# Two-block transformer on one core: last token rows turned inside the next part's first products, input loads reordered, output product in other PSUM banks

## The chip, the cores and the metric

The kernel runs on one core of a Trainium2 chip. The metric is the device time of one execution in microseconds, as the median of three runs; lower is better.

## The reference, cut to what matters

512 tokens of width 1024 go through a first block (a layer norm, then two layers, each a mixer followed by an MLP) and a second block (two layers over 16 meta tokens and the 512 tokens, 528 columns). What is computed at the places where one part follows another:

```python
x = layer_norm(x, ln0_g, ln0_b)
for l in range(DEPTH):                       # first block
    mix = hybrid_mixer(x, w_in[l], ...)      # ends with merged @ w_out[l]
    x = layer_norm(alpha * x + mix, ln1_g[l], ln1_b[l])
    hid = jnp.square(jax.nn.relu(x @ w_up[l]))
    x = layer_norm(alpha * x + hid @ w_down[l], ln2_g[l], ln2_b[l])
...
for l in range(DEPTH):                       # second block
    h = h + mixer2(rmsnorm(h, norm_g[l]), ...) @ w_out_2[l]
out = rmsnorm(h, final_g)
```

## The kernel before, in words

**Layout.** Between parts the tokens lie in rows: four tiles of 128 tokens by 1024 features, called token tiles 0 to 3 here (the second block has a fifth tile of 16 meta tokens, in front). A product needs them turned, features on the partitions: `to_features` (L190 to L197) turns one token tile with eight 128 by 128 transposes on TensorE (line L196) into two PSUM tiles. ScalarE rounds each into `xh` (L120), and VectorE writes the rest into `xl` (L121), so that a float32 product is three fast ones (xh by the high weight, xl by the high weight, xh by the low weight; `mm3`, line L107). Weights come by DMA into a ring of three buffers `wraw`, and `wsplit` makes the two parts: `whi` on ScalarE (L85), `wlo` on VectorE, or on GpSimd for the first tiles of a part (L87).

**Places where one part follows another.** The program is one long list, and the Tile compiler assigns buffers, waits and, by its own model of readiness, the order of each engine's queue. Where these places are:

- *Start* (`input_norm`, L278): x and the two layer norm rows (spread over 128 partitions by the DMA) are loaded, each token tile is normalized on VectorE (`layer_norm`: statistics L204, gain L210, bias L211) and turned, the parameter rows are loaded and turned (`params`, L325), and the first weights come after all that on the same DMA queue, SP's.
- *M0, M1* (`mixer` to `mlp`, layers 0 and 1): the mixer ends with `gated`, which multiplies each product by its gate (`th`, L576), adds to `acc` on GpSimd (L578) and splits the sum into `mh`, `ml`. The out product (L1000) then runs with tokens as output rows: its first 512 columns for all four token tiles while weights stream in, then its second 512 columns token tile by token tile, with residual add (L1004), layer norm and turning of each. The turning of token tile 3 comes after its layer norm.
- *O0, O1*: the beginning of that out product, behind the last products of `gated`. Its eight PSUM tiles are one ring of the pool `wop` (all eight banks). The mixer's product tiles `mm` are two banks of the pool `pm`, closed just before.
- *L0* (`mlp` to the next `mixer`) and *L1* (`mlp` to the second block): the down product (L1079) ends token tile by token tile in eight banks, with add (L1118), layer norm and turning. At L1 a root-mean-square norm (`rms`, L1151 to L1158) stands between.
- *P0* (second block, `project` of layer 0 to `feed` of layer 1): the same with L1686 and L1691, and `norm_tile`.

Each of the five then starts with `gemm_halves`: the first two weight tiles of the next part are multiplied with the first half of the token columns (256 of 512; 264 of 528 in the second block), then with the second half, 96 products in all. The first half reads token tiles 0 and 1 alone (and the meta rows).

```python
for h in range(2):                              # gemm_halves, L388
    hs = slice(256 * h, 256 * h + 256)
    for w, ps in zip(ws, tiles):
        self.b.mm3([(ps[:, hs], hs)], w, (self.xh, self.xl), nk, start=(h == 0))
```

- *N0, N1* (`latent` in the second block, L1395): five products of small width are normalized together. Two steps of another chain (`fox`: its q and k products) are handed out, and then, in two parts, a row of factors is spread (`rb`, L1440, VectorE), turned into PSUM (`bc`, L1444, TensorE) and multiplied in. `fox` goes on after both, with its v product. Products and `bc` share two PSUM buffers of two banks each.

In the mixers and the second block a planner written out in Python (`Weave`) decides the order in which chains of work are handed out: each chain yields an estimate of its TensorE time and of the delay until it can go on.

Of the kernel before, what the change touches and what calls it, by code (L numbers as in the profile page):

```python
# [15 lines left out]
P = 128  # L16
# [13 lines left out]
class B:  # L30
# [59 lines left out]
    def wstream(self, src, nk, c0, ntiles, m=P, spare=0):  # L90

        i = 0
        while i < ntiles:
            g = min(1024 // (nk * m), ntiles - i)
            raw = self.wload(src, nk, c0 + i * m, g * m)
# [118 lines left out]
def row_bcast(b, pool, vec, tag):  # L214
    t = b.t(pool, [P, vec.shape[0]], tag, bufs=1)
    b.nc.sync.dma_start(t, vec.unsqueeze(0).to_broadcast([P, vec.shape[0]]))
    return t


class First:  # L220


    def __init__(self, b, ctx, x_last):
        self.b, self.nc, self.a, self.tc = b, b.nc, b.a, b.tc
        nc, a, tc = self.nc, self.a, self.tc
        k1 = ctx.enter_context(tc.tile_pool(reuse_waits="tile", name="k1", bufs=1))
        self.res_d = [b.dp.tile([4, P, D], F32, name=f"res{i}") for i in range(DEPTH)]
        self.xh, self.xl = b.xh[:, :, :S], b.xl[:, :, :S]
        self.x_last = x_last
        self.PT = b.t(k1, [P, 95], "PT")  # L230
# [50 lines left out]
    def input_norm(self):  # L281
        b, nc, a, tc = self.b, self.nc, self.a, self.tc
        with ExitStack() as c2:
            tp = c2.enter_context(tc.tile_pool(reuse_waits="tile", name="ln0", bufs=1))
            pp = c2.enter_context(tc.tile_pool(reuse_waits="tile", name="ln0p", bufs=2, space=PSUM, side="right"))
            zs = [b.t(tp, [P, D], "z", bufs=4) for tt in range(4)]
            nc.sync.dma_start(zs[0], a["x"][0, 0:P, :])
            gb = row_bcast(b, tp, a["ln0_g"], "gb")
            bb = row_bcast(b, tp, a["ln0_b"], "bb")
            for tt in range(1, 4):  # L290
                nc.sync.dma_start(zs[tt], a["x"][0, tt * P : (tt + 1) * P, :])
            nc.sync.dma_start(b.ident, a["c_ident"])
            prm = self.params(0, tp, pp, "tr")
            next(prm)
            for tt, z in enumerate(zs):
# [302 lines left out]
    def low_rank(self, rp):  # L598
        b, nc = self.b, self.nc
        ws = b.wstream(self.w_in, KD, ZR + 1536, 3, spare=2)  # L600
        early = self.gemm_halves([next(ws), next(ws)])
# [343 lines left out]
    def mixer(self, l):  # L945
# [7 lines left out]
        accp = mctx.enter_context(tc.tile_pool(reuse_waits="tile", name=f"acc{l}", bufs=1))  # L953
        acc = b.t(accp, [P, KD, S], "acc")
# [36 lines left out]
        with ExitStack() as c2:  # L991
            wp = c2.enter_context(tc.tile_pool(reuse_waits="tile", name=f"wo{l}", bufs=1))
            pp = c2.enter_context(tc.tile_pool(reuse_waits="tile", name=f"wop{l}", bufs=8, space=PSUM))
# [34 lines left out]
            for tt in range(4):  # L1028
                pt = b.t(pp, [P, S], "b")
# [7 lines left out]
            to_features(b, pp, "b", x, self.xh, self.xl, tt * P)  # L1037
# [6 lines left out]
    def mlp(self, l):  # L1044
# [4 lines left out]
        with ExitStack() as c2:  # L1049
# [9 lines left out]
            with ExitStack() as c3:  # L1059
                self.pm = c3.enter_context(tc.tile_pool(reuse_waits="tile", name=f"up{l}", bufs=4, space=PSUM))  # L1060
                ws = b.wstream(a["w_up"][l], KD, 0, FF, spare=2)
                early = self.gemm_halves([next(ws), next(ws)])
# [41 lines left out]
            gb = row_bcast(b, hq, a["ln2_g"][l], "gb")  # L1104
            bb = row_bcast(b, hq, a["ln2_b"][l], "bb")
            if last:
                g2 = row_bcast(b, hq, a["norm_g_2"][0], "g2")
                norm_tile(b, hq, pp, "b", 4, g2)()
            for tt in range(4):
# [9 lines left out]
                layer_norm(b, hq, x, gb, bb, x)  # L1119
                if last:  # L1120
                    turn = norm_tile(b, hq, pp, "b", tt, g2)
                else:
                    nc.sync.dma_start(self.res_d[l + 1][tt], x)
                    turn = partial(to_features, b, pp, "b", x, self.xh, self.xl, tt * P)
            turn()
# [20 lines left out]
def rms(b, pool, h, n, gb, half=None):  # L1146
    nc = b.nc
    hn = b.t(pool, [P, D], "hn", bufs=2)
# [13 lines left out]
def norm_tile(b, pool, pp, tag, i, gb, half=None):  # L1162
    h, n, col = h_tile(b, i)
    hn = rms(b, pool, h, n, gb, half)
# [15 lines left out]
class Second:  # L1180
# [216 lines left out]
    def latent(self, l, cp, ps0, ws):  # L1397
# [40 lines left out]
        for part, tiles in ((0, range(3)), (1, range(3, 5))):  # L1438
# [11 lines left out]
            yield 1.2, 0.0  # L1450
# [216 lines left out]
    def project(self, l):  # L1667
# [3 lines left out]
        with ExitStack() as c2:  # L1671
# [55 lines left out]
            if turn:  # L1727
                turn()


def build(tc, a, out, stop=None, dbg=None):
    with ExitStack() as ctx:
# [11 lines left out]
        def open_residual():  # L1744
            hp = ctx.enter_context(tc.tile_pool(reuse_waits="tile", name="h2", bufs=1, side="right"))
            b.h_tok = b.t(hp, [P, 4, D], "htok")
            b.h_meta = b.t(hp, [NM, D], "hmeta")
            nc.sync.dma_start(b.h_meta, a["meta_tokens_2"])
# [90 lines left out]
```

## Time and profile before

| | |
|---|---|
| median of three runs | 3620.09 us (3615.1 to 3625.79) |
| the profiled execution, its own time | 3614.28 us |
| span in the trace | 3612.5 us |
| TensorE matmul busy | 3430.6 us (95%) |
| VectorE / ScalarE / GpSimd busy | 1891.6 / 1220.2 / 559.2 us |
| mean granted TensorE clock | 0.974 of full speed |

A trace row of the timeline has the start in us from the span's start, the duration, the engine, the source line and operation, output and inputs, and, in brackets, how long the engine had been idle before and what released it. A matmul's duration overlaps with the next one's, so work per product is read as the distance of starts, or from a stretch in which TensorE is never idle.

### The profile page before, as it was taken

The page shows a single profiled execution, that of the slowest core. Times are in us where ns is not written, and L with a number is a line of the kernel's source. Part 1 is how long each engine was busy: PE and PEld are TensorE (multiplying, and loading weights), DVE is VectorE, ACT ScalarE, POOL GpSimd, SP SyncE. Part 2 cuts the span into 40 slices and gives each one's busy share as a digit, 9 for nine tenths or more (in the row PEclk, how much of TensorE's full clock was granted, in tenths as well). Part 3 has the DMA queues.
Part 4 walks back from the last instruction along what each step waited for, and adds up shares of the span by engine and source line. Part 5 has one row for each costly group of instructions (what it writes and reads, how often), then busy time and mean ns, then how long its engine had stood idle before and what let it go on. Part 6 is the DMA issues. An engine that isn't in the chain of part 4 may idle for free. (4 is left out here: it accounts for less than half of the span.)

```text
span 3612.5 us, 56238 instructions
## 1 busy us (share of the span) xinstructions
PE 3430.6 (95%) x22346; PEld 2747.3 (76%) x22346; DVE 1891.6 (52%) x4547; ACT 1220.2 (34%) x2339; POOL 559.2 (15%) x660
## 2 busy tenths in 40 slices
PE   7999999999999989989989999899999999999998
PEld 5666676678887766667768888878989977787787
DVE  6576674552235556765552235465465355655634
ACT  2333342222223333423222223344333234443422
POOL 2221120222201211111122200110000111100011
PEclk9999999999999999999999999999999999999999
DMA  5422223333334322223342334122222332222232
GB/s 176 114 65 65 74 64 105 111 119 94 94 94 128 94 79 61 70 63 94 111 138 81 95 93 138 38 51 65 66 65 71 88 80 45 62 58 66 71 88 93
DMA packets 471832, 309.37 MB, mean 86 GB/s; under 512 B 105085, under 2 KB 433797, under 8 KB 471569
## 3 DMA queue, kind: packets, MB, share of 16 engines
q1 hardware_dynamic: 470992, 303.68, 30.0%
q8 instruction: 176, 2.88, 0.3%
q0 software_dynamic: 576, 2.10, 0.1%
q14 instruction: 88, 0.71, 0.1%
HBM read 280.76 MB, written 24.95 MB: 85 GB/s over the span
## 5 line engine op out<-in xcount | busy, mean ns | idle before, releaser
L107 PE MATMUL mm<-xh,whi 128*128 128x512 f32 (+2 forms) x3024 | 1002.9, 362 | 2.9 <-ACT whi L85 1.7
L107 PE MATMUL mm<-xh,wlo 128*128 128x512 f32 (+2 forms) x3024 | 969.4, 352 | 8.7 <-DVE wlo L87 7.3
L107 PE MATMUL mm<-xl,whi 128*128 128x512 f32 (+2 forms) x3024 | 972.7, 353 | 0.0
L87 DVE TENSOR_TENSOR wlo<-wraw,whi 128x1024 fp32r<-128x1024 f32 (+3 forms) x454 | 526.2, 1159 | 648.3 <-ACT whi L85 609.0
L85 ACT ACTIVATE whi<-wraw 128x1024 fp32r<-128x1024 f32 (+2 forms) x466 | 452.5, 971 | 1101.3 <-PE mm L107 835.6
L107 PEld LDWEIGHTS mm<-xh,whi 128*128 128x128 f32 x3024 | 540.9, 191 | 102.2 <-issue 23.5
L107 PEld LDWEIGHTS mm<-xh,wlo 128*128 128x128 f32 x3024 | 537.6, 191 | 85.8 <-DVE wlo L87 8.7
L107 PEld LDWEIGHTS mm<-xl,whi 128*128 128x128 f32 x3024 | 538.5, 191 | 72.6 <-issue 7.1
L1301 ACT ACTIVATE s<-s,nm 128x256 f32<-128x256 f32 (+5 forms) x216 | 116.2, 539 | 184.7 <-DVE nm L1299 180.3
L107 PE MATMUL mm<-yh,whi 128*128 128x512 f32 (+1 forms) x480 | 160.4, 368 | 10.0 <-ACT yh L120 5.3
L1079 PE MATMUL b<-whi,hh 128*128 128x512 f32 x416 | 164.6, 396 | 0.4 <-DVE PT L326 0.4
L1079 PE MATMUL b<-whi,hl 128*128 128x512 f32 x416 | 164.5, 396 | 0.0
L1079 PE MATMUL b<-wlo,hh 128*128 128x512 f32 x416 | 164.5, 395 | 0.0
L107 PE MATMUL mm<-yl,whi 128*128 128x512 f32 (+1 forms) x480 | 155.1, 356 | 4.9 <-DVE yl L121 4.9
L107 PE MATMUL mm<-yh,wlo 128*128 128x512 f32 (+1 forms) x480 | 154.0, 353 | 0.0
L1067 POOL TENSOR_TENSOR hid<-r 128x512 f32<-128x512 f32 x64 | 102.2, 1597 | 268.9 <-ACT r L1066 268.9
L121 DVE TENSOR_TENSOR hl<-hid,hh 128x512 fp32r<-128x512 f32 x64 | 43.3, 690 | 164.1 <-ACT hh L120 164.1
L817 DVE TENSOR_TENSOR cX<-cX,cT 128x60 f32<-128x60 f32 (+24 forms) x496 | 110.0, 222 | 12.1
L813 DVE TENSOR_TENSOR cT<-cX,cN 128x60 f32<-128x60 f32 (+24 forms) x496 | 109.5, 221 | 11.8
L107 PEld LDWEIGHTS mm<-yh,whi 128*128 128x128 f32 x480 | 84.2, 190 | 31.4 <-issue 7.7
L890 POOL TENSOR_TENSOR hp<-hist,pe 128x128 f32<-128x128 f32 x56 | 37.8, 675 | 432.3 <-DVE hist L894 185.7
L120 ACT ACTIVATE hh<-hid 128x512 fp32r<-128x512 f32 x64 | 39.3, 629 | 191.2 <-PE b L1079 184.4
(377 smaller groups left out, 5124.5 us busy)
## 6 DMA issues: line engine op xcount, KB each, us to landing
wraw<-in_w_in_dram SPq DMA_DIRECT2D x228, 512.0 KB
wraw<-in_w_up_dram SPq DMA_DIRECT2D x64, 512.0 KB
wraw<-in_w_down_dram SPq DMA_DIRECT2D x64, 512.0 KB
wraw<-in_w_branch_dram SPq DMA_DIRECT2D x48, 512.0 KB
wraw<-in_w_out_dram SPq DMA_DIRECT2D x32, 512.0 KB
g<-acc SPq DMA_DIRECT2D x32, 256.0 KB
cN<-nd SPq DMA_DIRECT2D x16, 512.0 KB
th<-g SPq DMA_DIRECT2D x32, 256.0 KB
```

The source lines that it names most:

```text
L85: self.nc.scalar.activation(out=wh, in_=rv, func=AF.Copy)
L87: eng.tensor_tensor(out=wl, in0=rv, in1=wh.bitcast(F32), op=ALU.subtract)
L107: self.nc.tensor.matmul(ps, lhsT=wt[:, k, :], rhs=xt[:, k, cs], start=(start and k == 0 and j == 0), stop=(k == nk - 1 and j == 2), skip_g ...
L120: nc.scalar.activation(out=hi, in_=ps, func=AF.Copy)
L121: nc.vector.tensor_tensor(out=lo, in0=ps, in1=hi.bitcast(F32), op=ALU.subtract)
L813: ins = nc.vector.tensor_tensor(out=tmp[:, :ni, :nt], in0=X[:, :ni, s_ : s_ + 1].to_broadcast([P, ni, nt]), in1=N[:, s_ : s_ + 1, s_ + 1 : ...
L817: nc.vector.tensor_tensor(out=X[:, :ni, s_ + 1 :], in0=X[:, :ni, s_ + 1 :], in1=tmp[:, :ni, :nt], op=ALU.subtract)
L890: nc.gpsimd.tensor_tensor(out=hp, in0=hist[:, cc - 1], in1=pe[:, :, c : c + 1].to_broadcast([P, 2, 64]), op=ALU.mult)
L1067: nc.gpsimd.tensor_tensor(out=hidden(m), in0=r, in1=r, op=ALU.mult)
L1079: nc.tensor.matmul(ps[tt, n], lhsT=x[:, tk], rhs=y[:, 0, ns], start=(k == 0 and j == 0), stop=(k == FF - 1 and j == 2))
L1301: nc.scalar.activation(out=ss[i][:n, :nk], in_=ss[i][:n, :nk], func=AF.Exp, bias=nm[:n, i : i + 1], accum_out=sm[:n, i : i + 1])
```

## The change

- The turning of the last token tile is not issued at the end of a part. It is kept (`self.turns`, `b.turn`) and issued between the two halves of `gemm_halves`, into a PSUM pool of the next part. At the start this holds for token tiles 2 and 3.
- So that the rows outlive their part, `acc` becomes a tile for the whole first block (16 KB in each partition) and its memory is also used as four token rows (`self.rows`): for x at the start, for token tile 3 after the first MLP, and in the MLPs for the layer norm rows and one scratch tile. A new tile `hn_last` holds token tile 3 at L1 and P0.
- At the start the DMA order is: identity, the two norm rows (4 KB each), x tiles 0 and 1, the first two weight tiles, x tiles 2 and 3, then the parameters. The norm rows are spread over the partitions by four float32 products with a row of ones, and stay in PSUM (four banks).
- The first four tiles of the out product and all turned tiles take banks of one pool, the second four of another (`wo2` opens first, then `wop`; four banks each).
- In `latent`, the third step of `fox` (its v product) is handed out between the two parts.

```diff
 def input_norm(self):
-            zs = [b.t(tp, [P, D], "z", bufs=4) for tt in range(4)]
-            nc.sync.dma_start(zs[0], a["x"][0, 0:P, :])
-            gb = row_bcast(b, tp, a["ln0_g"], "gb")
-            bb = row_bcast(b, tp, a["ln0_b"], "bb")
-            for tt in range(1, 4):
-                nc.sync.dma_start(zs[tt], a["x"][0, tt * P : (tt + 1) * P, :])
             nc.sync.dma_start(b.ident, a["c_ident"])
...
+                if tt == 2:
+                    self.raws = [b.wload(a["w_in"][0], KD, ZR + 1536 + i * P, P) for i in range(2)]
+                nc.sync.dma_start(self.rows[:, tt, :], a["x"][0, tt * P : (tt + 1) * P, :])
...
+            gb, bb = (b.t(pg, [P, D], f"g{i}") for i in range(2))
+            for v, ps in zip(rows, (gb, bb)):
+                for i in range(2):
+                    nc.tensor.matmul(ps[:, i * S : i * S + S], lhsT=one, rhs=v[:, i * S : i * S + S], start=True, stop=True)
...
-                to_features(b, pp, "tr", z, self.xh, self.xl, tt * P)
+                if tt < 2:
+                    to_features(b, pp, "tr", z, self.xh, self.xl, tt * P)
...
+        self.turns = [partial(to_features, src=self.rows[:, tt, :], xh=self.xh, xl=self.xl, col=tt * P) for tt in (2, 3)]

-    def gemm_halves(self, ws, nk=KD):
+    def gemm_halves(self, ws, pool, tag, nk=KD):
         for h in range(2):
+            if h:
+                for turn in self.turns:
+                    turn(self.b, pool, tag)
+                self.turns = []

 def mixer(self, l):
-            pp = c2.enter_context(tc.tile_pool(reuse_waits="tile", name=f"wop{l}", bufs=8, space=PSUM))
+            p2 = c2.enter_context(tc.tile_pool(reuse_waits="tile", name=f"wo2{l}", bufs=4, space=PSUM))
+            pp = c2.enter_context(tc.tile_pool(reuse_waits="tile", name=f"wop{l}", bufs=4, space=PSUM))
...
-                pt = b.t(pp, [P, S], "b")
+                pt = b.t(p2, [P, S], "b")
...
-            to_features(b, pp, "b", x, self.xh, self.xl, tt * P)
+            self.turns = [partial(to_features, src=x, xh=self.xh, xl=self.xl, col=tt * P)]

 def mlp(self, l):
-            turn()
+            if last:
+                b.turn = turn
+            else:
+                self.turns = [partial(to_features, src=xo, xh=self.xh, xl=self.xl, col=tt * P)]

 class Second, gemm_halves:
         for i in range(2):
+            if i:
+                self.b.turn(self.b, self.pa, "at")

 def latent:
-            yield 1.2, 0.0
+            yield (1.2, 0.0) if part else next(fox)

 def project:
-            if turn:
-                turn()
+            b.turn = turn
```

## Rows read from the trace of the kernel before

**Rows 1.** The page, busy time of each engine over the span.
```profile
PE 3430.6 (95%) x22346; PEld 2747.3 (76%) x22346; DVE 1891.6 (52%) x4547; ACT 1220.2 (34%) x2339; POOL 559.2 (15%) x660
```
**Rows 2.** Windows of TensorE: stretch, us, busy (instructions), granted clock, DMA share, GB/s.
```profile
0.00:44.30 44.30, 21.92 (x129) 1.00 0.64 197
724.00:752.52 28.52, 23.85 (x98) 0.94 0.70 237
777.68:795.90 18.22, 13.99 (x104) 0.91 0.04 11
1144.56:1162.30 17.74, 13.63 (x105) 0.90 0.22 70
1840.88:1870.62 29.74, 25.05 (x98) 0.89 0.67 227
1895.77:1914.89 19.12, 14.92 (x105) 0.82 0.00 1
2264.62:2287.10 22.48, 14.73 (x102) 0.77 0.01 1
2952.09:2968.15 16.06, 12.76 (x105) 1.00 0.02 2
2325.81:2342.97 17.16, 13.44 (x90) 0.90 0.12 11
782.98:786.10 3.12, 3.12 (x16) 0.50 0.05 14
787.00:795.00 8.00, 8.00 (x70) 1.00 0.01 2
754.60:763.60 9.00, 9.00 (x40) 1.00 0.59 163
```
**Rows 3.** Timeline: turning of the last token tile at M0, L0, M1, L1, P0.
```profile
781.88 1.46 PE L196 MATMUL b<-ident,xtok 128*128 128x128 f32 x8 [4.20 <-DVE xtok L211]
...
1148.67 1.97 PE L196 MATMUL b<-ident,xtok 128*128 128x128 f32 x8 [4.11 <-DVE xtok L211]
...
1899.97 1.94 PE L196 MATMUL b<-ident,htok 128*128 128x128 f32 x8 [4.20 <-DVE htok L211]
...
2272.38 1.94 PE L196 MATMUL b<-ident,hn 128*128 128x128 f32 x8 [7.75 <-DVE hn L1158]
...
2955.36 1.29 PE L196 MATMUL b<-ident,hn 128*128 128x128 f32 x8 [3.26 <-DVE hn L1158]
```
**Rows 4.** Timeline: VectorE's second step of turning, tile 3 at P0, tile 2 at L0.
```profile
2956.66 0.69 DVE L121 TENSOR_TENSOR xl<-b,xh 128x512 fp32r<-128x512 f32 x1 [0.78 <-ACT xh L120]
...
1145.06 1.27 DVE L121 TENSOR_TENSOR xl<-b,xh 128x512 fp32r<-128x512 f32 x2
```
**Rows 5.** Timeline at O0: first out product, splits of its first two weights.
```profile
720.83 1.22 DVE L87 TENSOR_TENSOR wlo<-wraw,whi 128x1024 fp32r<-128x1024 f32 x1
...
728.48 1.22 DVE L87 TENSOR_TENSOR wlo<-wraw,whi 128x1024 fp32r<-128x1024 f32 x1
...
728.71 0.77 PE L1000 MATMUL b<-whi,mh 128*128 128x512 f32 x1 [4.67 <-DVE th L576]
```
**Rows 6.** Timeline at N0: second part's spread on TensorE, and the v product.
```profile
2332.35 2.43 PE L1444 MATMUL mm<-ident,rb 128*128 128x128 f32 x10 [2.86 <-DVE rb L1440]
...
2334.72 0.81 PE L107 MATMUL mm<-xh,whi 128*128 128x264 f32 x2
```
**Rows 7.** Timeline of the start: statistics, weight splits, a held operation, a float32 product.
```profile
4.46 1.29 DVE L204 BATCH_NORM_STATS2 bst<-z 128x6 f32<-128x512 f32 x2 [3.16 <-DMA z<-in_x_dram]
...
24.79 5.23 POOL L87 TENSOR_TENSOR wlo<-wraw,whi 128x1024 fp32r<-128x1024 f32 x2
24.93 0.68 DVE L121 TENSOR_TENSOR xl<-tr,xh 128x512 fp32r<-128x512 f32 x1
...
25.53 5.05 DVE L211 SCALAR_TENSOR_TENSOR z<-z,lnr,bb 128x512 f32<-128x512 f32 x1
...
44.34 1.88 PE L262 MATMUL at<-oh,tab 32*4 32x512 f32 x4
```

More of the change, by code (lines that the diff above doesn't have):

```diff
@@ L94, in wstream @@
             g = min(1024 // (nk * m), ntiles - i)
-            raw = self.wload(src, nk, c0 + i * m, g * m)
+            raw = raws.pop(0) if raws else self.wload(src, nk, c0 + i * m, g * m)
             for j in range(g):
@@ L211, in layer_norm, with row_bcast @@
         nc.vector.scalar_tensor_tensor(out=x_out[:, cs], in0=z[:, cs], scalar=r, in1=bb[:, cs], op0=ALU.mult, op1=ALU.add)
-def row_bcast(b, pool, vec, tag):
-    t = b.t(pool, [P, vec.shape[0]], tag, bufs=1)
+def row_bcast(b, pool, vec, tag, t=None):
+    if t is None:
+        t = b.t(pool, [P, vec.shape[0]], tag, bufs=1)
     b.nc.sync.dma_start(t, vec.unsqueeze(0).to_broadcast([P, vec.shape[0]]))
@@ L229, in __init__ @@
         self.x_last = x_last
+        self.acc = b.t(ctx.enter_context(tc.tile_pool(reuse_waits="tile", name="acc", bufs=1)), [P, KD, S], "acc")
+        self.rows = self.acc.rearrange("p (t k) s -> p t (k s)", t=4)
         self.PT = b.t(k1, [P, 95], "PT")
@@ L599, in low_rank @@
         b, nc = self.b, self.nc
-        ws = b.wstream(self.w_in, KD, ZR + 1536, 3, spare=2)
-        early = self.gemm_halves([next(ws), next(ws)])
+        ws = b.wstream(self.w_in, KD, ZR + 1536, 3, spare=2, raws=self.raws)
+        early = self.gemm_halves([next(ws), next(ws)], self.pr, "sc")
         for i in range(3):
@@ L952, in mixer @@
         self.y_d = [b.dp.tile([P, 4, S], F32, name=f"y{l}{n}") for n in range(2)]
-        accp = mctx.enter_context(tc.tile_pool(reuse_waits="tile", name=f"acc{l}", bufs=1))
-        acc = b.t(accp, [P, KD, S], "acc")
+        acc = self.acc
         self.pm = mctx.enter_context(tc.tile_pool(reuse_waits="tile", name=f"pm{l}", bufs=2, space=PSUM))
@@ L1061, in mlp @@
                 ws = b.wstream(a["w_up"][l], KD, 0, FF, spare=2)
-                early = self.gemm_halves([next(ws), next(ws)])
+                early = self.gemm_halves([next(ws), next(ws)], self.pm, "mm")
                 for m in range(FF):
@@ L1103, in mlp @@
                 held.append((k, h, w))
-            gb = row_bcast(b, hq, a["ln2_g"][l], "gb")
-            bb = row_bcast(b, hq, a["ln2_b"][l], "bb")
+            spare = [self.rows[:, i, :] for i in range(4)]
+            gb = row_bcast(b, hq, a["ln2_g"][l], "gb", spare[0])
+            bb = row_bcast(b, hq, a["ln2_b"][l], "bb", spare[1])
             if last:
-                g2 = row_bcast(b, hq, a["norm_g_2"][0], "g2")
-                norm_tile(b, hq, pp, "b", 4, g2)()
+                g2 = row_bcast(b, hq, a["norm_g_2"][0], "g2", spare[2])
+                norm_tile(b, hq, pp, "b", 4, g2, None, spare[3])()
             for tt in range(4):
@@ L1118, in mlp @@
                     nc.vector.scalar_tensor_tensor(out=x[:, ns], in0=x[:, ns], scalar=ALPHA, in1=ps[tt, n], op0=ALU.mult, op1=ALU.add)
-                layer_norm(b, hq, x, gb, bb, x)
+                xo = x if last or tt < 3 else self.rows[:, tt, :]
+                layer_norm(b, hq, x, gb, bb, xo)
                 if last:
-                    turn = norm_tile(b, hq, pp, "b", tt, g2)
+                    turn = norm_tile(b, hq, pp, "b", tt, g2, None, b.hn_last if tt % 2 else spare[3])
                 else:
-                    nc.sync.dma_start(self.res_d[l + 1][tt], x)
-                    turn = partial(to_features, b, pp, "b", x, self.xh, self.xl, tt * P)
-            turn()
+                    nc.sync.dma_start(self.res_d[l + 1][tt], xo)
+                    turn = partial(to_features, b, pp, "b", xo, self.xh, self.xl, tt * P)
+            if last:
+                b.turn = turn
+            else:
+                self.turns = [partial(to_features, src=xo, xh=self.xh, xl=self.xl, col=tt * P)]
         self.xctx.close()
@@ L1143, in rms_half, with rms @@
     return v
-def rms(b, pool, h, n, gb, half=None):
+def rms(b, pool, h, n, gb, half=None, hn=None):
     nc = b.nc
-    hn = b.t(pool, [P, D], "hn", bufs=2)
+    if hn is None:
+        hn = b.t(pool, [P, D], "hn", bufs=2)
     ss = b.t(pool, [P, 1], "ss", bufs=2)
@@ L1159, in rms, with norm_tile @@
     return hn
-def norm_tile(b, pool, pp, tag, i, gb, half=None):
+def norm_tile(b, pool, pp, tag, i, gb, half=None, hn=None):
     h, n, col = h_tile(b, i)
-    hn = rms(b, pool, h, n, gb, half)
+    hn = rms(b, pool, h, n, gb, half, b.hn_last if i == 3 else hn)
+    if i == 3:
+        return partial(to_features, src=hn, xh=b.xh, xl=b.xl, col=col, n=n)
     return partial(to_features, b, pp, tag, hn, b.xh, b.xl, col, n)
@@ L1747, in open_residual @@
             b.h_meta = b.t(hp, [NM, D], "hmeta")
+            b.hn_last = b.t(hp, [P, D], "hnl")
             nc.sync.dma_start(b.h_meta, a["meta_tokens_2"])
```

15 lines of the change are left out of this document (13 added, 2 removed).

## The prediction

> **What bounds the kernel now.** The page first: TensorE is busy 95% of the span, VectorE 52% [rows 1]. So only time in which TensorE stands, or runs at its lower clock, can be won, and the next view is TensorE by stretches. Stepping through the span in 20 us windows, I looked for the ones with a low busy time or clock, and cut them to the places that the change touches [rows 2]. In rows 2 the third number of a line is busy time; what it lacks to the second is standing. The first line is the start (0 to 44.3, the end of the two early products); the next two are O0 and M0, then L0, then O1 and M1, then L1, P0, and N0. Last come three yardsticks: at M0 right after the wait the clock is 0.50 (1.2 GHz) and some 15 products of 256 columns start in 3.12 us, 0.21 each; later at full clock (2.4 GHz) 68 start in 8.00 us, 0.118 each; and 512-column products start every 0.233 us (9.00 / 38.6). (The counts include products that reach in from outside.) The five turnings of rows 3 show what TensorE waits for: the last token tile's norm on VectorE, 3.3 to 7.8 us.
>
> The stretch at a place minus its work at full clock is the most that the change can win there.
>
> **M0, L0, M1, L1, P0: the turning moves behind the first half.** Nothing is added or removed: eight transposes, two ACT and two DVE operations go from one end of 48 products to the other. The first half needs token tiles 0 and 1 only, and its weights were split long before, so it can start where TensorE falls idle (the left ends of rows 2). Work: 96 × 0.118 = 11.4 us (11.7 at 264 columns), eight transposes 0.8 (at M0 they end TensorE's distance that much later). What is late next is the second half: it now stands directly behind its transposes. At P0 these start at 2955.36 [rows 3], and the first `xl` is written at 2956.66 + 0.69 = 2957.35 [rows 4], 2.0 us later, when the second product of the half can go; without a wait it would go after 0.8 + 0.1. New gap: 1.1 us per place. It is too short to expect the lower clock behind it: after P0's 3.3 us of waiting the stretch still has 1.00 [rows 2].
> - M0: 11.4 + 0.8 + 1.1 = 13.3 against 18.2: **4.9**. The tile is ready at 781.88, before the first half ends (777.68 + 5.7).
> - M1: 13.3 against 19.1: **5.8**.
> - L0: here the first half's PSUM banks matter. In the down product's ring of eight banks the tile freed longest ago is taken first, and by that order token tile 2 is turned in banks 0 and 1, which the next part's products take. They then wait for its `xl`, until 1145.06 + 1.27 = 1146.33 [rows 4]: 1.8 us. The order is my reading of the code, no row shows it; bounds 0 and 1.8, and I take 1.8, as the code says. 15.1 against 17.7: **2.6**.
> - L1: the tile is ready only at 2272.38 [rows 3], later than the first half can end (2264.62 + 5.8, even with 1.8 of bank wait). So 2272.38 + 0.8 + 1.1 + 5.9 = 2280.2 against 2287.1: **6.9**. The norm chain on DVE, ACT and POOL sets that time and is not moved.
> - P0: 11.7 + 0.8 + 1.1 = 13.6 against 16.1. A bank wait is possible (0 to 1.6); I take the middle, as nothing tells which bank it is: **1.7**.
>
> Together 21.9. The last tile's turn also leaves the old part's PSUM pool; nothing else queues behind it on PE. On ACT and DVE its splits now stand behind no new work, since the weights' splits of the first two tiles are done.
>
> **O0, O1: other banks.** The first out product waits 4.67 us for the last gate operation on VectorE [rows 5], though it does not read its result: the ring's first bank held the mixer's last product. In the new pool the first four tiles lie in the upper banks, which the mixer gave up long ago. The weights of its first 24 products are ready (720.83 + 1.22), so it starts at 724.0. It takes 5.6 us, to 729.6; the next weights' low part ends at 728.48 + 1.22 = 729.70 [rows 5], needed from the second product on, at 729.8: just in time. Then 96 × 0.233 = 22.4 against 28.5 and 29.7 [rows 2]: **6.1** and **7.3** (wait plus products at the lower clock). What is late next: the DMA, 0.70 busy and 237 GB/s in the stretch [rows 2]. If the second columns' weights came late, up to all 6 could be given back; I take none, since only their last quarter is needed more than 4 us into the second columns.
>
> **N0, N1: the v product between the two parts.** TensorE waits 2.86 us for the second part's factors and then runs its ten spreads in 2.43 us [rows 6], with the clock at 0.90 in the stretch [rows 2]. The v product (24 pairs, some 5.9 us) has its weights by then and fits there; the second spread then finds its factors ready. Less standing, less slow clock: 2.86 + about 1.0 of slow spread + 0.7 at the lower clock = 4.6 at best. Against it: two PSUM buffers serve spreads, v and the next product, which must now wait until the second part's two tiles are multiplied in, two DVE operations of 512 columns, 2 × 0.68 by the size of [rows 7]'s, 1.3 us. **3.3** each, 6.6 in all; bounds 0 and 4.6. In SP's queue nothing moves.
>
> **The start.** On SP's queue two 512 KB spreads of norm rows become two loads of 4 KB, the identity moves to the front, and two weight loads move ahead of x tiles 2 and 3, the 12 parameter loads, the lambda row and the constants. Now the early products end at 44.30, half of the stretch standing [rows 2]. What will set the end is VectorE: per token tile statistics 1.29, about 0.4 of small steps, gain and bias 1.4 each, and 1.3 for `xl`, 5.8 us, 23.2 for four. It starts when x tile 0 lands: 4.46 now [rows 7], some 5.2 behind the small loads. Norm rows through PSUM: L262 shows 1.88 for two such products [rows 7], so 3.8 for four, twice that at the lower clock; VectorE needs the second row some 6 us after it starts, so this costs 0 to 2, I take 1. Turning token tiles 2 and 3 then needs banks that the norm rows hold until tile 3's bias is added; the two-tile ring serializes four groups, some 1.5 us more. So the second half starts near 5.2 + 23.2 + 1 + 1.5 = 30.9 and ends 5.7 to 6.5 later, about 37.3: **7.0** (bounds 3 and 11). On PE the four products stand ahead of the transposes that wait for x anyway; the parameters' later landing is covered by the first half.
>
> One price here is open. The bias step that took 5.05 us began while GpSimd split weights for 5.23 us; in the same time an operation with one operand in PSUM took 0.68 [rows 7]. With the norm rows in PSUM, gain and bias are of the second kind, so I count no such hold; held, they would cost up to 4.3, and the start would win 2.7. The Trainium skill (SBUF — State Buffer, Who interferes with whom) has the rule: a VectorE operation with two SBUF inputs shuts out, or is shut out by, a GpSimd one that reads SBUF, whichever comes first, and one with a single SBUF input does neither. By it the start keeps its 7.0; by the wider bound it wins 2.7.
>
> **Costed at nothing:** norm rows and scratch in the memory of `acc` (in the MLPs their loads and readers are far apart), the copy-free output of token tile 3 into it, and 16 KB less free SBUF.
>
> **Sum.** 21.9 + 13.4 + 6.6 + 7.0 = 48.9 us. From the profiled execution, 3614.3, that leaves 3565.4. The median of the runs shown is 5.8 above the profiled one, so I forecast **3571**.
>
> **The rivals.**
> 1. *The order or the banks undo the seams.* The compiler places instructions by its own readiness model; if it puts the turning ahead of the first half again, or the first half waits for PSUM at all five places, the 21.9 are gone: 3593. For it: the bank order at L0 and P0. Against it: at the start it already put first-half products ahead of turnings.
> 2. *The first mixers do not pass the time on.* If the recurrence on VectorE sets a mixer's length, start and L0 (9.6) vanish: 3581. Against it: VectorE is at 52%, TensorE at 95% [rows 1].
> 3. *Slower: the second block's order gets worse.* The planner counts one step of 1.2 us less and 5.4 earlier in `latent`, so everything after it is handed out at other moments: 12 heads' pairs by 5 query tiles in 2 layers, 120 pieces of attention. If each left TensorE standing 0.5 us more, that is 60 us: 3631. It decides from 0.4 us on, where the 48.9 are eaten. Against it: the largest wait of this kind now, at N0, is 2.86 us, and most stretches there are fully busy.
> 4. *Better:* no bank waits, best N and start: 1.8 + 0.8 + 2.6 + 4 more, 3562.
>
> **How the numbers follow.** Forecast 0.62 (its own range 3560 to 3583), rival 1 0.18, rival 2 0.08, rival 4 0.06, rival 3 0.06. A measurement of this kernel tells 0.3%, 10.9 us, from no change. Faster by more needs under 3609: all but rival 3 (0.06) and a small part of rival 1 (0.02, if the DMA also takes O0 and O1). Of these 0.08, half would end within the bound and half above it: faster 0.92, same 0.04, slower 0.04. The range takes in rival 1 with a few us of spread, and the bounds below: 3555 to 3600.
>
> **What would show it.** Right: L196 of the last tile stands after 48 products of the next part at all five places, with about 1 us before the second half and the clock near 1.00 in those stretches; L1000 starts within 0.5 us of the last L107; no wait at L1444; the third early product starts near 38 us. Wrong: waits of L1000 for weights, of first halves for `xl`, more waits of L1317 or L1332 in the second block, or a DVE operation of about 5 us at the start.

## The result, and the profile after

The changed kernel took **3568.14 us** (median of 4 runs, 3565.18 to 3570.96) against 3617.60 us for the kernel before, measured beside it (4 runs, 3607.41 to 3625.79): ratio 0.9865, 95% interval 0.9836 to 0.9893. The forecast was 3571 (3555 to 3600). Two later comparisons with the same kernel gave 3566.18 against 3620.74 (0.9852, 0.9836 to 0.9868) and 3562.08 against 3617.32 (0.9848, 0.9822 to 0.9873). The medians fell by 49 to 55 us. One of the ten executions of `b_banks`, a variant below, took 4688.57 us, with a granted clock of 0.16 from 3340 us to its end: the ratio is taken without it, and the trace, which is of it, is read below only up to 1900 us.

The profiled execution took 3570.74 us, its span is 3569.0. On the page TensorE's busy time is only 3.0 us less than in [rows 1], while the span fell by 43.5. That does not make the gain standing time alone: at the start TensorE has 5.1 us more to do (27.00 against 21.92 us busy, since the four spreads of the norm rows are new) and in the mixers its busy time rose (below), while at O0, M0, L0, O1, M1 and L1 it fell by 0.5 to 2.4 us each.

```profile
PE 3427.6 (96%) x22354; PEld 2739.3 (77%) x22354; DVE 1887.6 (53%) x4548; ACT 1219.5 (34%) x2339; POOL 557.1 (16%) x660
```

The next view answers to [rows 2]: windows of TensorE in the changed kernel (stretch, us, busy, granted clock, DMA share, GB/s), for the start, O0, M0, L0, O1, M1, L1, P0, and the middle of N0 from the first spread to the end of the second.

```profile
0.00:36.31 36.31, 27.00 (x137) 1.00 0.65 211
721.35:743.96 22.61, 22.61 (x97) 1.00 0.83 289
768.87:782.16 13.29, 12.82 (x108) 1.00 0.05 15
1130.60:1145.40 14.80, 13.10 (x107) 1.00 0.15 50
1830.53:1853.14 22.61, 22.61 (x97) 1.00 0.86 292
1878.05:1891.34 13.29, 12.82 (x108) 1.00 0.00 1
2240.14:2255.83 15.69, 13.67 (x107) 1.00 0.29 90
2915.89:2930.68 14.79, 13.43 (x109) 1.00 0.02 2
2295.26:2305.44 10.18, 9.72 (x77) 1.00 0.21 21
```

The clock is 1.00 (2.4 GHz) in every line, where [rows 2] had 0.77 to 0.94 in most. For the start the record and the products disagree: up to 22.5 us products of 256 columns start every 0.21 us, the distance that [rows 2] shows at 0.50, and every 0.12 us after that. M0 and M1 take 13.29 us; the forecast said 13.3. At the start waits of 2.87 and 1.62 us are left; elsewhere what is left of waiting is short. The timeline of TensorE at M0, L0, L1 and N0 of the changed kernel:

```profile
774.52 0.28 PE L107 MATMUL mm<-xh,wlo 128*128 128x256 f32 x1
774.64 1.03 PE L196 MATMUL mm<-ident,xtok 128*128 128x128 f32 x8
775.92 0.51 PE L107 MATMUL mm<-xh,whi 128*128 128x256 f32 x2 [0.25 <-ACT xh L120]
776.65 0.39 PE L107 MATMUL mm<-xl,whi 128*128 128x256 f32 x1 [0.22 <-DVE xl L121]
...
1132.07 0.39 PE L107 MATMUL mm<-xh,whi 128*128 128x256 f32 x1 [1.23 <-DVE xl L121]
...
1146.75 0.47 PE L107 MATMUL mm<-xh,whi 128*128 128x512 f32 x1 [1.20 <-DVE sq L426]
...
2241.61 0.34 PE L107 MATMUL mm<-xh,whi 128*72 128x264 f32 x1 [1.22 <-DVE xl L121]
...
2248.16 1.29 PE L196 MATMUL at<-ident,hnl 128*128 128x128 f32 x8 [0.48 <-DVE hnl L1186]
...
2295.26 1.37 PE L1477 MATMUL mm<-ident,rb 128*128 128x128 f32 x10
...
2303.53 1.38 PE L1477 MATMUL mm<-ident,rb 128*128 128x128 f32 x10
```

The last tile's eight transposes stand between the halves and wait for nothing, where [rows 3] had 3.3 to 7.8 us; behind them TensorE waits 0.25 + 0.22 = 0.47 us, and the first product with `xl` starts 776.65 - 774.64 = 2.01 us after the transposes do (2.0 was said). At L0 and L1 the first half waits for an `xl` (1.23 and 1.22 us), which the prediction reads as a wait for a PSUM bank, and at P0 too (0.98, at 2917.11). At L1 the tile is still 0.48 us late. At N0 the second spread runs in 1.38 us without a wait, where [rows 6] had 2.43 after 2.86.

How much of this reaches the end is seen by subtracting the start of one and the same instruction in the two traces. The difference is called the lead. The columns are the start before, the start after, the lead, and what the lead grew by since the line above:

```
third product after the start    46.15    38.21    7.94    +7.9  start
gated product late in mixer 0   714.55   712.02    2.53    -5.4  mixer 0
out product after O0            754.61   746.06    8.55    +6.0  O0
first up product after M0       795.90   782.16   13.74    +5.2  M0
third product after L0         1163.49  1146.75   16.74    +3.0  L0
gated product late in mixer 1  1828.97  1818.78   10.19    -6.6  mixer 1
out product after O1           1889.06  1871.59   17.47    +7.3  O1
first up product after M1      1914.90  1891.34   23.56    +6.1  M1
last down product              2263.34  2239.12   24.22    +0.7  MLP 1
gate transpose after L1        2287.57  2257.38   30.19    +6.0  L1
product behind N0              2427.83  2391.92   35.91    +5.7  N0
out product before P0          2941.61  2905.65   35.96     0.0  second block, layer 0
first scores after P0          3007.62  2970.32   37.30    +1.3  P0
products behind N1             3152.30  3108.86   43.44    +6.1  N1
```

The ten places gave 54.6 us, the two mixers took 12.0 back. What those 12.0 us are, and which part of the change wins what, is the matter of the experiments.

### The profile page after: what moved, and what is told of

The parts are those of the page before. It is cut to its first block, busy times and chain, and to the rows that moved or that the text cites. A ratio compares the mean times of both kernels' runs of the same rounds, so it can differ in the third digit from the quotient of the medians.

```text
span 3569.0 us, 56259 instructions
## 1 busy us (share of the span) xinstructions
PE 3427.6 (96%) x22354; PEld 2739.3 (77%) x22354; DVE 1887.6 (53%) x4548; ACT 1219.5 (34%) x2339; POOL 557.1 (16%) x660
## 5 line engine op out<-in xcount | busy, mean ns | idle before, releaser
L107 PE MATMUL mm<-xh,whi 128*128 128x512 f32 (+2 forms) x3024 | 997.8, 361 | 8.9 <-DVE xl L121 3.4
L107 PE MATMUL mm<-xh,wlo 128*128 128x512 f32 (+2 forms) x3024 | 965.7, 350 | 7.2 <-DVE wlo L87 6.9
L107 PE MATMUL mm<-xl,whi 128*128 128x512 f32 (+2 forms) x3024 | 968.9, 351 | 1.4 <-DVE xl L121 1.4
L107 PEld LDWEIGHTS mm<-xh,whi 128*128 128x128 f32 x3024 | 536.5, 190 | 110.8 <-issue 23.2
L107 PEld LDWEIGHTS mm<-xh,wlo 128*128 128x128 f32 x3024 | 534.5, 190 | 84.0 <-DVE wlo L87 8.7
L107 PEld LDWEIGHTS mm<-xl,whi 128*128 128x128 f32 x3024 | 534.6, 189 | 75.1 <-issue 6.9
L107 PE MATMUL mm<-yh,whi 128*128 128x512 f32 (+1 forms) x480 | 161.1, 369 | 10.0 <-ACT yh L120 5.3
L107 PE MATMUL mm<-yl,whi 128*128 128x512 f32 (+1 forms) x480 | 155.4, 356 | 4.5 <-DVE yl L121 4.5
L107 PE MATMUL mm<-yh,wlo 128*128 128x512 f32 (+1 forms) x480 | 154.6, 355 | 0.0
L107 PEld LDWEIGHTS mm<-yh,whi 128*128 128x128 f32 x480 | 84.4, 190 | 31.4 <-issue 7.7
```

What stands on the lines that cost most here:

```text
L107: self.nc.tensor.matmul(ps, lhsT=wt[:, k, :], rhs=xt[:, k, cs], start=(start and k == 0 and j == 0), stop=(k == nk - 1 and j == 2), skip_g ...
```

## The experiments

**Is the mixers' loss a property of the change?** The changed kernel again, and the kernel before again, unedited.

> The changed kernel once more, for the lengths of the two mixers (from the end of the early products, 36.3, to the first out product, and from the end of L0 to O1). In the first pair of traces they took 685.0 and 685.1 us after the change, 679.7 and 678.5 before it. Theory (the extra 12 us are bouts of the lower clock that fall differently in every execution): the lengths move by 2 us or more from the first trace of the same kernel, at other places, and each place outside the mixers is within 0.3 us of the first trace. Rival A (the mixers take back what comes early, since a chain of their own sets their end): both lengths are again 685 within 1 us, with the losses at the same places (at 486 to 496, 1306 to 1330, 1756 to 1777).

> The kernel before once more. Theory (mixer lengths are chance): mixer 0 and mixer 1, 679.7 and 678.5 us in the first trace of this kernel, move by 2 us or more, while O0, M0, L0, O1, M1 and L1 stay within 0.3 us, but for one that a bout of the lower clock reaches. Rival A (the mixers of the kernel before are shorter because they start later): 679 and 678 again within 1 us.

Measured: `same` 3566.18 us, `same_before` 3612.63 us (one run). Windows of TensorE over mixer 0, from the third early product to a gated product late in it, 4740 products each, in five executions: before, `same_before`, after, and two variants from below whose code up to O0 is the changed kernel's, `u_turns` and `u_both`:

```profile
46.94:721.52 674.58, 629.48 (x4740) 0.95 0.32 90
```
```profile
46.27:726.54 680.27, 634.79 (x4740) 0.94 0.31 89
```
```profile
39.00:719.00 680.00, 633.27 (x4740) 0.95 0.32 91
```
```profile
38.92:714.12 675.20, 631.12 (x4740) 0.95 0.32 92
```
```profile
38.85:709.56 670.71, 627.24 (x4740) 0.96 0.32 92
```

The same early start goes with 680.0, 675.2 and 670.7 us, the same late start with 674.6 and 680.3. The products are the same 4740, yet their busy time runs from 627.2 to 634.8 us, while the standing time, the rest of each line, runs from 43.5 to 46.7 only. Mixer 1 took 674.64 us in the first trace of the kernel before, 670.32 in the second, 681.20 after the change and 675.32 in `u_turns`. So the 12.0 us are no fixed price of the change: the lengths move by 5 to 10 us from execution to execution. An average price of some us is not excluded. From the third early product to the late gated product, the two traces of the kernel before and that of `b_banks` have 667.9 to 674.1 us in mixer 0 and 661.2 to 665.5 in mixer 1; the changed kernel and its variants below up to `rows_sbuf`, nine traces, have 664.5 to 675.3 and 662.2 to 675.5. The theory had expected `same` to differ by 2 us or more in both mixers; it differed by 0.3 in the first and 3.3 in the second, so alone it would have proved little. `same_before` bore it out: the mixers moved by 5.7 and 4.3 us, O0, M0 and L0 by 0.1 at most, O1 and M1 by 1.1 and 0.9. One cause can be seen: the granted clock. In the next lines the first two are the same work in mixer 0, in the trace of after and in that of `u_turns`; the last two are the end of the early products, in after and in `same`:

```profile
487.52:497.17 9.65, 9.65 (x85) 0.51 0.15 34
```
```profile
485.14:492.68 7.54, 7.54 (x89) 0.76 0.13 20
```
```profile
31.00:36.30 5.30, 5.30 (x46) 1.00 0.00 2
```
```profile
31.00:36.30 5.30, 5.30 (x34) 0.71 0.00 0
```

TensorE never stands in them. One execution is granted the lower level (1.2 GHz) for a stretch in which another is not. The instructions before the second pair are the same, but their times are not: in `same` the products came at their closer distance from 20.4 us on, in the changed kernel's first trace from 22.5, and TensorE then stood longer before the last two turnings. First the changed kernel, then `same`:

```profile
28.72 1.25 PE L196 MATMUL sc<-ident,acc 128*128 128x128 f32 x8 [1.62 <-DVE xl L121]
```
```profile
25.68 1.09 PE L196 MATMUL sc<-ident,acc 128*128 128x128 f32 x8 [0.34 <-DVE acc L210]
28.64 1.25 PE L196 MATMUL sc<-ident,acc 128*128 128x128 f32 x8 [1.87 <-DVE xl L121]
```

In `u_banks`, which has the same code there, the closer distance came at 20.3 us, the two waits were 0.37 and 1.87, and the clock was 0.72 from 31.0 to 36.3. In `u_latent` it came at 21.0, with 0.14 and 1.86, and the clock stayed at 1.00. What went before a fall in the mixers was not followed.

**The start alone undone.**

```diff
-            gb, bb = (b.t(pg, [P, D], f"g{i}") for i in range(2))
...
+            gb = row_bcast(b, tp, a["ln0_g"], "gb")
+            bb = row_bcast(b, tp, a["ln0_b"], "bb")
...
+                to_features(b, pp, "tr", z, self.xh, self.xl, tt * P)
...
+        self.turns, self.raws = [], None
```

> The start as before the change, all else kept. Theory: the early products end near 44.3 again instead of 36.3, the mixer passes that on but for the chance of its clock, and the median is 8 us above the changed kernel's, about 3576 (3572 to 3580). Rival A (the mixer's own chain sets its end): the first out product starts where it does now, 721, and the time is at most 2.6 us longer. A DVE operation of about 5 us beside the GpSimd splits comes back.

Measured: 3570.42 us (3560.84 to 3578.00, 4 runs), ratio to before 0.9862 (0.9840 to 0.9884), 4.2 us above `same`. In its trace the third early product starts 7.8 us later than in the changed kernel's, and the mixer ends 5.4 us later. The long bias step of [rows 7] is back, with 5.06 us (at 25.53). The 5.4 are not Rival A's 2.6, but with mixers that move by 5 us neither a median of four runs nor one trace can say how much of the 7.9 arrives; the readings are 4.2 and 5.4.

**The turning alone undone**, at M0, M1, L0, L1 and P0.

```diff
-            self.turns = [partial(to_features, src=x, xh=self.xh, xl=self.xl, col=tt * P)]
+            to_features(b, pp, "b", x, self.xh, self.xl, tt * P)
...
             if last:
-                b.turn = turn
+                turn(b, pp, "b")
+                b.turn = lambda *_: None
             else:
-                self.turns = [partial(to_features, src=xo, xh=self.xh, xl=self.xl, col=tt * P)]
+                turn()
```

> The last token tile is turned at the end of its part again at all five places; start, banks and the order of the second block kept. Theory: the stretches of the changed kernel grow back by 4.9 (M0), 5.8 (M1), 3.0 (L0), 6.8 (L1) and 1.5 (P0), 22.0 us in all: about 3590. Rival A: L0's 3.0 are taken back by the second mixer, 3587. Rival B (the gain of the seams comes from the extra banks or the order elsewhere, not from the turning): under 3580.

Measured: 3575.40 us (0.9876, 0.9859 to 0.9892), 9.2 above `same`, not 22, and under Rival B's bound: for M0 and M1 the rival was right. L0 grew by 3.5 us, the stretch from L1 to the end of N0 by 5.4 and P0 by 2.9 (leads as above), but M0 and M1 shrank by 0.7 and 0.8. The timeline of M0 in `u_turns`, and then its window:

```profile
768.07 0.28 PE L107 MATMUL mm<-xl,whi 128*128 128x256 f32 x1
768.43 0.63 PE L196 MATMUL b<-ident,xtok 128*128 128x128 f32 x4
768.82 0.36 PE L107 MATMUL mm<-xh,wlo 128*128 128x256 f32 x1
769.02 0.28 PE L107 MATMUL mm<-xh,whi 128*128 128x256 f32 x1
769.14 0.60 PE L196 MATMUL b<-ident,xtok 128*128 128x128 f32 x4
```
```profile
763.98:776.57 12.59, 12.51 (x108) 1.00 0.06 16
```

The code turns the tile ahead of the first half, yet the compiler has set both groups of transposes among the first half's products, with products between them, so that the wait of 0.47 is gone: 12.6 us against 13.3. At M0 and M1 the moved turning is not what wins.

**The banks alone undone, both undone, and the banks alone done.** The edit is the same line in the three: one ring of eight in place of two of four (or, from the kernel before, the reverse).

```diff
-            p2 = c2.enter_context(tc.tile_pool(reuse_waits="tile", name=f"wo2{l}", bufs=4, space=PSUM))
-            pp = c2.enter_context(tc.tile_pool(reuse_waits="tile", name=f"wop{l}", bufs=4, space=PSUM))
+            pp = p2 = c2.enter_context(tc.tile_pool(reuse_waits="tile", name=f"wop{l}", bufs=8, space=PSUM))
```

> The out products of the first block draw all their tiles from one ring of eight banks again, all else kept. Theory: the first out product waits for the last gate operation again, some 4.7 us, and runs on at the lower clock for a while; O0 and O1 grow back by 6.0 and 7.3 us: about 3581. Rival B (the wait went because the mixer now ends otherwise): no wait of L1022 on DVE, under 3573.

> Turning at the end of the parts and one ring of eight banks together, start and second-block order kept. With either alone undone, M0 and M1 kept their 13.3 us. Theory (either part is enough there: what the first products of the next part need is a bank that the last turning does not use, and then the compiler itself sets them ahead of it): M0 and M1 take 18.2 and 19.1 us again, 4.9 and 5.8 more than the changed kernel; with O0 and O1 (13.3) and L0, L1, P0 (9) the time is 33 us above the changed kernel's, about 3599. Rival (M0 and M1 were won by something else that stays, such as the earlier clock or the output of the norm elsewhere): they keep 13.3, about 3588.

> The kernel before with the split of the out product's banks alone (two rings of four). Theory: O0 and O1 win 6.0 and 7.3, and M0 and M1 win 5.6 and 6.6 with no line of the turning moved, 25 us in all: the time of before less 25, about 3594. Rival (the turning must be moved in the code for the M places): 13 us, about 3606.

Measured: `u_banks` 3581.22 us (0.9884, 0.9865 to 0.9902), 15.0 above `same`; `u_both` 3599.64 us (0.9956, 0.9937 to 0.9974), against 3599 expected; `b_banks` 3603.77 us (0.9959, 0.9945 to 0.9973), 14.1 under the kernel before. In `u_banks` the wait of [rows 5] is back, O0 costs 6.2 us and O1 7.3 by the leads, and M0 and M1 change by 0.0. In `u_both` the leads give 5.2 us each for M0 and M1. There the last turning stands ahead of all products again, with the wait of [rows 3], and M0 takes [rows 2]'s 18.2 us. First the row of `u_banks` at O0, then those of `u_both` at M0:

```profile
726.93 0.77 PE L1021 MATMUL b<-whi,mh 128*128 128x512 f32 x1 [4.70 <-DVE th L598]
```
```profile
769.96 1.44 PE L196 MATMUL b<-ident,xtok 128*128 128x128 f32 x8 [4.20 <-DVE xtok L211]
```
```profile
765.50:783.70 18.20, 13.96 (x105) 0.91 0.04 11
```

`u_turns` and `u_both` differ by the rings alone, `u_banks` and `u_both` by the turning alone. So at M0 and M1 **either part is enough**, and only with both gone are the 10 us lost. Which bank stands in the way, no row shows: that the first half needs one which the last turning uses is a reading. `b_banks` shows the same from the other side: with no line of the turning moved, the last tile's transposes stand among the first half's products, and M0 takes 12.6 us (M1 12.5):

```profile
776.97 0.63 PE L196 MATMUL b<-ident,xtok 128*128 128x128 f32 x4
777.67 0.60 PE L196 MATMUL b<-ident,xtok 128*128 128x128 f32 x4
```
```profile
772.50:785.10 12.60, 12.52 (x108) 1.00 0.06 16
```

By leads over the kernel before, its two out products and M places win 22 us, 25 expected: its O0 wins 4.5 and O1 5.2 only. At each of the two TensorE waits 0.95 us for a split of weights; at O0 the DMA's share is 1.00 beside it (735 to 740 us). The median has 14 of the 22, which is nearer to the rival's 13; it is the trace of M0 and M1 that speaks against the rival, and what the rest of the median's 8 us is was not followed (the mixers' scatter is as large).

**The `latent` step alone undone.**

```diff
-            yield (1.2, 0.0) if part else next(fox)
+            yield 1.2, 0.0
```

> The v product stands behind both parts of the latent norm again, all else kept. Theory by the two traces: TensorE waits for the second factors again and runs their spreads at the lower clock; N0 costs 4.7 to 5.4 and N1 6.1, 11 us in all, about 3577. By the prediction's term 6.6 us, about 3573. Rival (the planner's other order of the attention pieces gives or takes as much): the stretch of N0 and N1 does not account for the difference, and the rest of each second-block layer changes by 2 us or more.

Measured: 3574.10 us (0.9889, 0.9873 to 0.9906), 7.9 above `same`. The wait of [rows 6] returns to N0, to the hundredth:

```profile
2293.68 2.58 PE L1477 MATMUL mm<-ident,rb 128*128 128x128 f32 x10 [2.86 <-DVE rb L1473]
```

By the leads N0 costs 5.7 us and N1 6.0, 11.7 together; at 7.9 the median is between this and the prediction's 6.6 and decides for neither. (`same` is from another comparison; by the two ratios to the kernel before, 0.9889 and 0.9852, the difference is some 13 us.) Outside N0 and N1 layer 0 differs only at the start of `project`, by 2.6 us, and there the same two waits (1.44 and 1.35 us) stand in both traces, but behind them this execution was granted a clock of 0.69 where the changed kernel's had 1.00. In `u_turns` and `u_banks`, which keep the changed kernel's order, the same stretch is longer too, by 1.3 and 1.5 us. So it is the clock that scatters and not the planner's order that tells, and the rival is not borne out.

**The start's norm rows in SBUF.** The rows go from PSUM to SBUF by ScalarE, so that gain and bias have two SBUF operands again.

```diff
+            sb = [b.t(tp, [P, D], f"n{i}") for i in range(2)]
+            for o, ps in zip(sb, (gb, bb)):
+                nc.scalar.activation(out=o, in_=ps, func=AF.Copy)
+            gb, bb = sb
```

> The changed kernel's start with the two norm rows copied by ScalarE from PSUM into SBUF, so that the gain and bias steps on VectorE have two SBUF operands, as before the change. If such an operation and a GpSimd one shut each other out: the GpSimd splits of the weights (13.85 to 18.5 in the changed kernel, 2.3 us each) and the gain and bias steps beside them (0.74 each there) no longer run together, a VectorE step of 2 to 5 us or a split that starts later or takes that much longer appears, and the second half of the early products (36.3) ends 2 to 4 us later. If they do not: all steps keep 0.7, and the end moves by no more than the copies on ScalarE cost, 1 to 2 us.

Measured: 3566.66 us (one run; its early products ended 5.1 us later, 2 to 4 expected, and its mixer was 3.6 shorter). VectorE and GpSimd at the start, first in the changed kernel, then in `rows_sbuf`:

```profile
13.85 4.67 POOL L87 TENSOR_TENSOR wlo<-wraw,whi 128x1024 fp32r<-128x1024 f32 x2
14.99 0.74 DVE L211 SCALAR_TENSOR_TENSOR acc<-acc,lnr,g 128x512 f32<-128x512 f32 x1
15.64 0.74 DVE L210 SCALAR_TENSOR_TENSOR acc<-acc,bmv,g 128x512 f32<-128x512 f32 x1
```
```profile
12.55 2.84 DVE L210 SCALAR_TENSOR_TENSOR acc<-acc,bmv,n 128x512 f32<-128x512 f32 x1
15.31 3.19 DVE L210 SCALAR_TENSOR_TENSOR acc<-acc,bmv,n 128x512 f32<-128x512 f32 x1
12.14 2.69 POOL L87 TENSOR_TENSOR wlo<-wraw,whi 128x1024 fp32r<-128x1024 f32 x1 [2.19 <-ACT whi L85]
15.59 2.35 POOL L87 TENSOR_TENSOR wlo<-wraw,whi 128x1024 fp32r<-128x1024 f32 x1
```

With one operand in PSUM the steps take 0.74 beside the splits. With both in SBUF two of them take 2.84 and 3.19, and each ends 0.56 us after a split does (14.83 and 17.94). The start then wins 7.9 - 5.1 = 2.8 us; for held steps the prediction had 2.7. The Trainium skill (SBUF — State Buffer, Who interferes with whom) says that a VectorE operation with two SBUF inputs and a GpSimd one that reads SBUF shut each other out, and one with a single SBUF input does not; both traces agree. Who is held does not follow the starts in these rows: the second step starts 0.28 us before the second split, and the step is the one that is held.

**A version with three more edits.** M0 and M1 turned at once in the code, as in `u_turns`; tile 2 of L0 turned in the banks of its own sums; the third product of `low_rank` in a bank of the other ring.

```diff
-        ps = b.t(pp, [P, 4, P], tag)
+        ps = own[g].rearrange("p (j c) -> p j c", j=4) if own else b.t(pp, [P, 4, P], tag)
...
-                    turn = partial(to_features, b, pp, "b", xo, self.xh, self.xl, tt * P)
+                    turn = partial(to_features, b, pp, "b", xo, self.xh, self.xl, tt * P, own=(ps[tt, 0], ps[tt, 1]))
...
-            ps = early[i] if i < 2 else self.gemm_tile(next(ws))
+            if i < 2:
+                ps = early[i]
+            else:
+                ps = b.t(self.pr, [P, S], "sc")
+                b.mm3([(ps, slice(0, S))], next(ws), (self.xh, self.xl), KD)
```

> The changed kernel with three edits: at M0 and M1 the last tile is turned at once in the code, so that the compiler places it (0.7 and 0.8 won when the turning was undone); token tile 2 of L0 is turned in the banks of its own sums, not in those of the next part's first products (their wait of 1.2 us should go); the third product after the start and after L0 takes a bank of the other ring (waits of 1.9 and 1.2 us should go). Theory: 1.5 + 1.2 + 3.1 = 5.8 us less than the changed kernel, about 3561, if the mixers pass on what comes early; 1.5 to 2 us less if not, about 3565. If the bank reading of L0 is wrong, its first product still waits for xl.

> The version with the three further edits again, beside the changed kernel on the same chip. Theory from the traces: M0 and M1 0.7 each, L0's two waits of 1.2 each, nothing at the start, since the gap there was filled by another product: 3.8 us. If the 12 us between the medians of the last two comparisons are real, its mixers are again 6 us or more shorter than the changed kernel's, each; if they were chance, the medians differ by 3 to 6 us.

> The changed kernel a third time, as the yardstick for the version with the three further edits: median 3567 (3564 to 3571), mixers anywhere from 676 to 687 us.

Measured: `best` 3554.18 us (0.9832, 0.9816 to 0.9848), 7 us under the 3561 expected; `best2` 3558.44 (0.9847, 0.9816 to 0.9878), and beside it `same2` 3562.08 (0.9848, 0.9822 to 0.9873), under the 3564 to 3571 expected. At L0 of `best` the first half follows the turning of tile 2 at once, and the waits of 1.23 and 1.20 are gone:

```profile
1124.28 1.03 PE L196 MATMUL b<-ident,xtok 128*128 128x128 f32 x8
1125.07 0.36 PE L107 MATMUL mm<-xh,whi 128*128 128x256 f32 x1
...
1138.32 0.39 PE L107 MATMUL sc<-xh,whi 128*128 128x512 f32 x1
```

From there to the third product L0 takes 13.25 us against 1146.75 - 1130.60 = 16.15. So the prediction's reading of the banks at L0 was right: the same `xl` is still written there, and only the bank of its transposes is another. At L1 and P0 the reading was not tested. By leads the three places give 0.7, 0.8 and 2.9 us in both traces, 4.4; at the start the third product comes 1.9 earlier and wins nothing, because the changed kernel had a constant's product in that gap. Beside `same2` the median is 3.6 lower, as the places say, but the intervals overlap, so that the total is not shown. The 12 us between the medians of `best` and `same` are from two comparisons (by the ratios 7 us) and do not return beside `same2`. From the end of the early products, mixer 0 of `best2` was 4.0 us shorter than in the first trace of the changed kernel and its mixer 1 6.1, where `best2`'s text expected 6 or more in each if the 12 us were real; `u_both` had 9.3 in mixer 0 without those edits.

## Why the prediction was right, and where not

- **The main idea held**: the time is that of TensorE's standing and slow stretches, each place but N0 and N1 ended within 1 us of where the working put it, and outside the start no new wait over 1.3 us came at any of them. Of the signs named, the last tile stands behind 48 products at all five places, the clock is 1.00 in all of them, L1022 starts 0.23 us after the last L107 starts, L1477 has no wait, the third early product starts at 38.21 (38 was said). Of the signs against it one came, at the size that the working allowed for: first halves wait for `xl` at L0, L1 and P0. That is as far as Rival 1 came true.
- **The sum was 6 us short**: 48.9 said, 54.6 by leads, 49 to 55 by medians. M, L, O and P: 35.3 said (21.9 and 13.4), 34.9 by leads. The start: 7.0 said, 7.9; its second half begins at 30.07 us (30.9 said), and the four spreads take 3.75 + 3.62 us, the doubled price that the working named. That the first comparison showed 49.5 us, close to the sum, is partly luck: the places gave 54.6, and the first two traces differ by 43.5.
- **The mis-sized term is N0 and N1**: 3.3 each said, "4.6 at best", 5.7 and 6.1 measured. The 1.3 us that were set against it, for the two PSUM buffers, did not appear: in the kernel after nothing waits between v and the second spread or just behind it, and a wait of 0.40 us that the kernel before had behind its v product (L1242, at 2342.45) is gone too. At N1 the lower clock also had more to give back: the clock before was 0.66 from 3010 to 3020 us, 3.4 us lost, where [rows 2]'s stretch of N0 lost 17.16 × 0.10 = 1.7, as the working took.
- **The step that failed** is "The turning moves behind the first half" as the cause at M0 and M1. The size was right (4.9 and 5.8 said, 5.2 and 6.1 by leads), but `u_turns` shows the same gain with the turning left where it was, and `u_both`, against `u_turns`, that one ring of eight had kept it from coming. The prediction counted the split of the banks for O0 and O1 only. So it is the banks that carry 13.3 us alone (O0 and O1) and 10 to 11 more as one of two sufficient edits; the moved turning is needed at L0, L1 and P0, some 10 us by leads (3.0 + 6.0 + 1.3; `u_turns` lost 3.5, 5.4 and 2.9 there).
- **L0 and the gap**: L0 lost 1.23 us to the bank wait (1.8 taken). The gap of 1.1 per place was right: M0's 13.29 less 11.4 of products and 0.8 of transposes leaves 1.1. The timeline calls only 0.47 of it idle. Most of the rest are ends that otherwise lie under the next start: the eight transposes last 1.03 us in place of 0.8, the two products that need no `xl` 0.51 in place of 0.24. P0 gave 1.3 (1.7 taken), with a bank wait of 0.98 (0.8 taken).
- **Rival 2**, the mixers that do not pass the time on, looked right in the first pair of traces (12.0 us gone) and does not stand as a mechanism: the same loss and its opposite come and go with one and the same kernel. How much of the start's 7.9 and L0's 3.0 arrives on average stays open within the mixers' scatter.
- **Rival 3** did not happen: layer 0 of the second block behind N0 changes by 0.0 us.

## What to carry to other kernels

When the compiler orders instructions by readiness, ask of every seam which buffer, not which line of code, keeps the next part back: at M0 and M1 two rings of four banks in place of one of eight did as much as moving the work by hand. Undo parts one at a time and then together: two edits that each suffice look worthless alone and are worth 10 to 11 us as a pair. And before a loss elsewhere is explained, profile the unchanged kernel again: stretches that move by 5 to 10 us by themselves can hide or make up a gain of that size, while the places that were edited repeat within 0.3 us when the clock does.

## What the runs showed of the hardware that was not expected

- In executions with the same instructions the full clock came at different times at the start: products of 256 columns went from a distance of 0.21 us to 0.12 at 20.3 us in `u_banks`, 22.5 in the first trace of the changed kernel and 23.4 in `u_both`. In the two where it came first (`u_banks`, and `same` at 20.4) the clock then fell to 0.72 and 0.71 for the 5.3 us from 31.0 on, with TensorE busy throughout; in the first trace it was 1.00 there. In the mixers such stretches, with others not followed, go with 670 to 681 us for the same work.
- A VectorE step of 0.74 us with two SBUF operands that meets GpSimd splits ends only behind them, and splits that follow one another can hold it through two: in [rows 7] one step took 5.05 us beside a pair of splits (5.23 us), in `rows_sbuf` two steps took 2.84 and 3.19 us beside one split each.
